# A down projection in which 8 of 22 k-tile pairs are multiplied as 2x2 blocks with seven products

## The chip, the cores and the metric

The kernel runs on one core of a Trainium2 chip. The metric is device time of one execution in microseconds (us), here the median of three runs. Engines are named as in the profile: PE is TensorE, PEld its weight loads, DVE VectorE, ACT ScalarE, POOL GpSimd, and SP the engine that issues most DMAs.

## The reference

A decoder trunk of two layers on 256 tokens with 2048 channels. Each layer has a token mixer and a SwiGLU feed-forward part (D_FF = 5632), each between two norms. What matters here is the feed-forward part, the last step of each layer:

```python
def swiglu(u, w_gu, w_down):
    gu = u @ w_gu
    return (jax.nn.silu(gu[..., :D_FF]) * gu[..., D_FF:]) @ w_down
...
        x = x + rmsnorm(o, g[1])
        x = x + rmsnorm(swiglu(rmsnorm(x, g[2]), ffn_w_gu[l], ffn_w_down[l]), g[3])
```

With h = silu(..) * (..) of shape 256 x 5632, the down projection is h @ w_down, 256 x 5632 times 5632 x 2048, once per layer.

## The kernel before

**Precision.** Every large product is taken in three matmuls. A float32 number is split into hi, its rounding to the type float32r, and lo, the rest, and a product is hi*hi + lo*hi + hi*lo. ACT writes hi (line 193), DVE subtracts to get lo (line 194). For the activations this is done when they are produced (class `XT`, which holds one page for each pair of k-tiles, with hi and lo of both); for the weights it is done as they stream through.

**Weight units.** All weights are cut in units of 128 x 1024 float32 (512 KB), listed in the order of use by `_unit_list`. `take` hands out the next unit as a pair of pages (hi, lo). Before that it issues, in the program's order, what lies ahead: `dma_one` loads a unit on SP's queue into a "raw" page, `split_one` turns a raw page into hi and lo and frees it. `take` starts a load while fewer than three (at its end four) raws are unsplit and `room(1)` holds, and up to two splits while at most `look` units are ahead (4 in layer 0's feed-forward part, 8 in layer 1's) and `room(2)` holds. `room(n)` asks for `st["res"] + n` free pages; `res` is 2 in the gate/up part and 0 in the down projection. Where nothing was split ahead, `take` splits the unit at that moment, behind everything already queued on ACT and DVE.

**Pages and banks.** There are 44 pages of 4 KB per partition. The free list is first in, first out, so a new tile takes the page that has been free for longest, and its first writer waits on the chip for that page's last reader. PSUM has eight banks, kept in the same way.

**Side work.** Matmul loops call `tick` twice after each three matmuls of a unit of the feed-forward part (eight ticks per unit). `tick` advances generators that were handed to `spawn`; a `yield n` puts one off by n ticks. All engines execute in the program's order, so what a generator emits between two units stands between them in the queues of ACT, DVE and PE.

**The feed-forward part** is `ffn`. X (tile `xf`, 8 pages) is the normed x. Gate/up: for each of 22 pairs f2 of k-tiles of h, eight units of `x_unit` (2 k-tiles x 2 row blocks x 3 matmuls, 128 x 512 columns each) fill two banks, and `gu_evac` is spawned: Silu on ACT (799), the product on DVE (801), eight ticks later four transposes (808), two ticks later hi and lo of the pair in `hT` (812, 813). The first two pairs share one loop. Then X is freed and the down projection runs over four chunks c of 512 columns. For each it takes 22 units, one for each pair, into two banks (row blocks t = 0, 1). `Tail.chunk` evacuates a chunk: on ACT a Square with its row sum (563), on DVE the product with the gain row into `og` (567). The gain rows `gb` (two pages) come over POOL's queue. In the last chunk pages of hT are dropped one by one, `step(u)` runs layer 0's preparation of the next stage (memory rows loaded on POOL's queue, new tiles for the next X), and the last four units (`HOLD`) are taken together, so that row block 0 is finished ahead of row block 1 (`Tail.last`). `rstd_of` makes the norm's factor (DVE, then POOL), `Tail.residual` adds to x (597), and in layer 1 `store` writes the output.

**x.** The residual stream x is four pages of 128 x 1024 float32. It stays in SBUF all the time. `next_x` adds the residual of row block 1, transposes x into the next X, and squares x for the next norm.

## Time and profile before

| | |
|---|---|
| median of three runs | 2556.76 us (2556.6 to 2558.26) |
| the profiled execution, its own time | 2556.86 us |
| its span | 2555.1 us |
| mean granted clock of TensorE | 0.997 |
| matmuls of the two down projections | 704 in each of lines 330, 331, 332 |

The span goes from the first to the last instruction; the rest of the execution's time lies around it. A row of the profile's groups reads: line, engine, operation, output<-inputs, shapes, count | busy us, mean ns | idle time of the engine just ahead of them, and what ended it. In rows of a timeline the first number is the start in us, the second the length; a bracket gives the idle time ahead and its releaser. In rows of waits the engine and line on the left waited for those on the right: us in total, times, longest us.

### The profile page before, as it was taken

To read this page: it belongs to the slowest core of one execution; us is meant where nothing else is said; L and a number is where in the kernel's file an instruction comes from. 1 tells how busy PE (TensorE), PEld (TensorE's weight loads), DVE (VectorE), ACT (ScalarE), POOL (GpSimd) and SP (SyncE) were. 2 spreads that over 40 slices of the span, in tenths; PEclk is the share of its full clock that TensorE was granted. 3 is DMA by queue.
4 is the path that set the end of the run, shared out by engine and by line. 5 is a ranking of instruction groups with operands and counts; after the bars stand their busy time and mean duration, and the time that the engine had idled before them with its cause. 6 is when DMAs were issued, how large, how long until landed. Compare 5 with 4: busy or idle time off the path is not lost.

```text
span 2555.1 us, 32090 instructions
## 1 busy us (share of the span) xinstructions
PE 2522.1 (99%) x12326; PEld 2137.7 (84%) x12326; DVE 1449.6 (57%) x1926; ACT 1203.3 (47%) x1704; POOL 58.5 (2%) x73
## 2 busy tenths in 40 slices
PE   8999999999999999999999999999899999999998
PEld 6899999988888888888888888888788888888887
DVE  8564655557445554444457866896544444444444
ACT  7444444456434444444445555565444444444442
POOL 5000000000000000000000000000000000000000
PEclk9999999999999999999999999999999999999999
DMA  8455555576555555566676675346455555556664
GB/s 305 148 181 173 166 166 173 172 246 223 177 183 181 185 187 170 173 209 192 194 233 216 220 245 193 116 142 235 158 175 181 181 174 173 181 173 219 193 190 156
DMA packets 136010, 482.84 MB, mean 189 GB/s; under 512 B 15408, under 2 KB 15408, under 8 KB 135856
## 3 DMA queue, kind: packets, MB, share of 16 engines
q1 hardware_dynamic: 131904, 468.67, 56.8%
q0 software_dynamic: 3232, 11.01, 1.3%
q8 instruction: 96, 1.57, 0.3%
q10 hardware_dynamic: 720, 1.11, 0.1%
q14 instruction: 58, 0.48, 0.1%
HBM read 478.63 MB, written 2.10 MB: 188 GB/s over the span
## 4 chain that ended last, share of the span: by engine, by line
PE 93%; DVE 4%; ACT 2%; issue 1%; DMA 0%; POOL 0%; SPq 0%; DVEq 0%; ACTq 0%; POOLq 0%
PE bk L331 23%; PE bk L332 23%; PE bk L330 23%; PE bk L295 12%; PE bk L297 6%; DVE lo L194 2%; ACT hi L193 1%; PE sk L808 1%; PE sk L500 1%; PE bk L939 1%; PE bk L938 1%; PE sk L540 0%; PE bk L294 0%; PE sk L1123 0%; DVE x L597 0%
## 5 line engine op out<-in xcount | busy, mean ns | idle before, releaser
L194 DVE TENSOR_TENSOR lo<-raw,hi 128x1024 fp32r<-128x1024 f32 (+2 forms) x899 | 1061.6, 1205 | 613.0 <-ACT hi L193 575.6
L193 ACT ACTIVATE hi<-raw 128x1024 fp32r<-128x1024 f32 (+2 forms) x899 | 906.9, 1039 | 499.5 <-PE bk L331 239.3
L330 PE MATMUL bk<-hi,xf 128*128 128x512 f32 x1408 | 554.0, 393 | 0.6 <-ACT xf L383 0.6
L332 PE MATMUL bk<-lo,xf 128*128 128x512 f32 x1408 | 549.3, 390 | 0.0
L331 PE MATMUL bk<-hi,xf 128*128 128x512 f32 x1408 | 548.9, 390 | 0.0
L295 PE MATMUL bk<-xT,hi 128*128 128x512 f32 x1104 | 398.7, 404 | 0.0
L332 PEld LDWEIGHTS bk<-lo,xf 128*128 128x128 f32 x1408 | 265.0, 188 | 55.7
L330 PEld LDWEIGHTS bk<-hi,xf 128*128 128x128 f32 x1408 | 265.1, 188 | 54.1 <-ACT xf L383 1.0
L331 PEld LDWEIGHTS bk<-hi,xf 128*128 128x128 f32 x1408 | 265.3, 188 | 53.5 <-DVE xf L384 0.2
L297 PE MATMUL bk<-xT,lo 128*128 128x256 f32 x1035 | 289.6, 280 | 0.0
L330 PE MATMUL bk<-hi,hT 128*128 128x512 f32 x704 | 274.1, 389 | 0.0
L332 PE MATMUL bk<-lo,hT 128*128 128x512 f32 x704 | 273.9, 389 | 0.0
L331 PE MATMUL bk<-hi,hT 128*128 128x512 f32 x704 | 273.9, 389 | 0.0
L295 PEld LDWEIGHTS bk<-xT,hi 128*128 128x128 f32 x1104 | 204.1, 188 | 39.8 <-issue 0.2
L297 PEld LDWEIGHTS bk<-xT,lo 128*128 128x128 f32 x1035 | 195.5, 189 | 3.1
L331 PEld LDWEIGHTS bk<-hi,hT 128*128 128x128 f32 x704 | 132.2, 188 | 27.6
L330 PEld LDWEIGHTS bk<-hi,hT 128*128 128x128 f32 x704 | 132.2, 188 | 27.3
L332 PEld LDWEIGHTS bk<-lo,hT 128*128 128x128 f32 x704 | 132.2, 188 | 27.3
L801 DVE SCALAR_TENSOR_TENSOR ev<-bk,r_f,ev 128x256 f32<-128x256 f32 x88 | 42.2, 483 | 136.7 <-ACT ev L799 127.8
L799 ACT ACTIVATE ev<-bk,r_f 128x256 f32<-128x256 f32 x88 | 41.5, 474 | 164.9 <-PE bk L332 163.8
L322 ACT ACTIVATE ev<-bk 128x256 f32<-128x256 f32 x93 | 35.5, 382 | 129.7 <-PE bk L295 129.6
L295 PE MATMUL bk<-kT,hi 128*128 128x512 f32 x256 | 91.6, 399 | 0.0
(210 smaller groups left out, 2486.6 us busy)
## 6 DMA issues: line engine op xcount, KB each, us to landing
raw<-in_gu SPq DMA_DIRECT2D x352, 512.0 KB, 3.6
raw<-in_dn SPq DMA_DIRECT2D x176, 512.0 KB, 4.3
raw<-in_a_qk SPq DMA_DIRECT2D x96, 512.0 KB, 4.0
raw<-in_a_v SPq DMA_DIRECT2D x64, 384.0 KB, 3.0
raw<-in_cw SPq DMA_DIRECT2D x32, 512.0 KB, 4.6
raw<-in_b_out SPq DMA_DIRECT2D x32, 512.0 KB, 3.7
raw<-in_a_out SPq DMA_DIRECT2D x24, 512.0 KB, 4.4
raw<-in_b_q SPq DMA_DIRECT2D x24, 512.0 KB, 3.7
```

The source lines that it names most:

```text
L193: nc.scalar.activation(hi[1][:, s], r[:, s], AF.Copy)
L194: nc.vector.tensor_tensor(out=lo[1][:, s], in0=r[:, s], in1=hi[1][:, s].bitcast(F32), op=OP.subtract)
L295: mm(pt[:, :], lhsT=hi[:, ks], rhs=X.hl(kt), start=first, stop=last)
L297: mm(pt[:, S:], lhsT=lo[:, ks], rhs=X.part(kt, 0), start=False, stop=False)
L322: nc.scalar.activation(t1, pt[1][:, S:], AF.Copy)
L330: mm(p[:, :w], lhsT=xh, rhs=u[0][1][:, ws], start=f, stop=False)
L331: mm(p[:, :w], lhsT=xl, rhs=u[0][1][:, ws], start=False, stop=False)
L332: mm(p[:, :w], lhsT=xh, rhs=u[1][1][:, ws], start=False, stop=l)
L500: mm(s[:, o:o + n], lhsT=q[1][:, g, t * P:(t + 1) * P], rhs=k[1][:, g, :n], start=True, stop=True)
L799: nc.scalar.activation(g, pts[t][1][:, :S], AF.Silu, scale=r)
L801: nc.vector.scalar_tensor_tensor(h, pts[t][1][:, S:], r, g, op0=OP.mult, op1=OP.mult)
L808: nc.tensor.transpose(p[:, k * S + t * P:k * S + (t + 1) * P], hs[t][:, k * P:(k + 1) * P], ident)
```

## The change

Of the 22 pairs of k-tiles, the last 8 (`DN_S`, pairs 14 to 21) are multiplied differently. For two column chunks at a time (`cp`, a half of the columns) such a pair is a product of 2x2 blocks: two row blocks by two k-tiles, times two k-tiles by two column chunks. It is computed with seven block products P1 to P7 in place of eight (each is still three matmuls), from sums of blocks on both sides.

- On the activations' side `s_parts` makes four sums of 128 x 128 blocks from the transposes' bank at the end of `gu_evac`, splits them, and keeps them in one more page per pair (`Sp`) until the second half is through.
- On the weights' side a pair and half need the units of both chunks (kinds "a" and "b") and two combined units made on DVE ("T13", "T24"). `split_one` makes hi and lo of the unit a, one page with hi and lo of a half of b, and the pages T13 and T24 from differences and sums.
- The seven products are summed over all eight pairs in banks P1 to P7. The 14 other pairs add to P2 and P4 (chunk a) and to P3 and Q (chunk b), so eight banks are in use. After the last block step `sums` combines the banks on DVE into four SBUF tiles (two pages `ut`), and `block` adds P2, P3, P4 or Q to them ahead of the Square and the gain product, which now read SBUF.
- The order of units in a half mixes block steps with plain steps (`_dn_steps`): in the first half a0 to a4, then pair 14, and so on with two or three plain steps between two block steps, and six plain steps behind the last; in the second half a0 to a3 first, mostly two plain steps between two block steps, and ten behind the last, of which the last four are held as before.
- x is written to DRAM in `next_x` ahead of the feed-forward part (four DMAs on SP), its pages are freed, and it is read back at steps 8 to 11 of the second half. `og` and `gb` pages are taken when first needed, `Sp` and hT pages are dropped one by one in the second half. `res` is 3 in the down projection.

The diff, cut to its core:

```diff
+DN_S = tuple(range(14, FT // 2))
...
+    std = [u for u in range(FT // 2) if u not in DN_S]
+    a, b, q = [("a", u) for u in std], [("b", u) for u in std], [("S", u) for u in DN_S]
+    if cp == 0:
+        head, mix, tail = a[:4], [e for p in zip(a[4:], b) for e in p] + b[len(a) - 4:], []
+        tail, mix = mix[-4:], mix[:-4]
+    else:
+        head, mix, tail = a[:3], a[3:] + b[:6], b[6:]
+    return head + _weave(mix, q, 0) + tail
...
     def split_one():
...
+        if kd == "b":
+            ai, ra = kept["T24"]
+            hl = pages.get([P, UNIT], F32R, "hl", True)
+            split_ap(r[:, Bk], hl[1][:, A], hl[1][:, Bk])
+            ti, t = pages.get([P, UNIT], F32, "t13", True)
+            nc.vector.tensor_tensor(out=t[:, A], in0=r[:, A], in1=ra[:, A], op=OP.subtract)
+            nc.vector.tensor_tensor(out=t[:, Bk], in0=r[:, Bk], in1=r[:, A], op=OP.subtract)
...
+        if kd == "T13":
+            ai, ra = kept["T24"]
+            nc.vector.tensor_tensor(out=ra[:, A], in0=r[:, Bk], in1=ra[:, A], op=OP.add)
+            nc.vector.tensor_tensor(out=ra[:, Bk], in0=ra[:, Bk], in1=ra[:, A], op=OP.subtract)
...
         for s in halves(u, w):
-            nc.scalar.activation(hi[1][:, s], r[:, s], AF.Copy)
-            nc.vector.tensor_tensor(out=lo[1][:, s], in0=r[:, s], in1=hi[1][:, s].bitcast(F32), op=OP.subtract)
-        pages.put(ri, True)
+            split_ap(r[:, s], hi[1][:, s], lo[1][:, s])
+        if kd == "a":
+            kept["T24"] = (ri, r)
+        else:
+            pages.put(ri, True)
...
+        if name == "f":
+            for i in range(4):
+                nc.sync.dma_start(out=x_out[i], in_=x[i][1])
+                pages.put(x[i][0])
...
+    def s_parts(A):
+        sv = tmp.tile([P, 4, P], F32, tag="sv", name="sv")
+        sp = pages.get([P, 4, 2, P], F32R, "sp")
+        tt = nc.vector.tensor_tensor
+        s1 = tmp.tile([P, P], F32, tag="s11", name="s11")
+        nc.scalar.activation(s1, A[:, 0, 1], AF.Copy)
+        tt(out=sv[:, 0], in0=A[:, 1, 1], in1=s1, op=OP.add)
+        tt(out=sv[:, 1], in0=sv[:, 0], in1=A[:, 0, 0], op=OP.subtract)
+        tt(out=sv[:, 2], in0=A[:, 0, 0], in1=s1, op=OP.subtract)
+        tt(out=sv[:, 3], in0=A[:, 1, 0], in1=sv[:, 1], op=OP.subtract)
+        yield 1
+        nc.scalar.activation(sp[1][:, :, 0, :], sv, AF.Copy)
+        nc.vector.tensor_tensor(out=sp[1][:, :, 1, :], in0=sv, in1=sp[1][:, :, 0, :].bitcast(F32), op=OP.subtract)
+        return sp
...
+        if f2 in DN_S:
+            Sp[f2] = yield from s_parts(p.rearrange("p (k t q) -> p k t q", k=2, t=2))
         banks.put(b)
...
-        st["res"] = 0
+        st["res"] = 3
...
+            def quad(u):
+                A, Bk = slice(0, 512), slice(512, 1024)
+                sp = [[Sp[u][1][:, j, i, :] for i in range(2)] for j in range(4)]
+                w = take(f"dn{l}")
+                prod("P1", act(2 * u, 0), w[0][1][:, A], w[1][1][:, A])
+                prod("P2", act(2 * u + 1, 0), w[0][1][:, Bk], w[1][1][:, Bk])
+                give(w)
+                w = take(f"dn{l}")
+                prod("P3", sp[3], w[0][1][:, A], w[0][1][:, Bk])
+                give(w)
+                w = take(f"dn{l}")
+                prod("P5", sp[0], w[0][1][:, A], w[1][1][:, A])
+                prod("P7", sp[2], w[0][1][:, Bk], w[1][1][:, Bk])
+                give(w)
+                w = take(f"dn{l}")
+                prod("P6", sp[1], w[0][1][:, A], w[1][1][:, A])
+                prod("P4", act(2 * u + 1, 1), w[0][1][:, Bk], w[1][1][:, Bk])
+                give(w)
...
+            def sums():
+                yield 12
+                tp = [pages.get([P, 2, 512], F32, "ut") for _ in range(2)]
...
+                nc.scalar.activation(s1, bk["P1"][1], AF.Copy)
+                tt(out=u2, in0=bk["P6"][1], in1=s1, op=OP.add)
+                tt(out=u3, in0=bk["P7"][1], in1=u2, op=OP.add)
+                yield 2
+                tt(out=v, in0=bk["P5"][1], in1=u3, op=OP.add)
+                tt(out=u2, in0=bk["P5"][1], in1=u2, op=OP.add)
...
+            def block(key, pre=None):
+                c, t, s_ = T["c"][key]
+                nc.vector.tensor_tensor(out=s_, in0=bk[key][1], in1=s_, op=OP.add)
+                free(key)
+                tail.rows(2 * cp + c, t, s_, pre)
...
+                    if 8 <= steps < 12:
+                        i = steps - 8
+                        x[i] = pages.get([P, 1024], F32, "x")
+                        nc.sync.dma_start(out=x[i][1], in_=x_out[i])
...
+            if cp == 0:
+                tail.gain(1)
+                spawn(blocks_of(("P2", "P3", "P4", "Q")))
+            else:
+                last_units(plan[-HOLD:])
```

`prod` issues the three matmuls of one product and calls `tick` twice. `tail.rows` is the body of the former `Tail.chunk` for one row block: Square on ACT, the norm's factor where asked for, the gain product on DVE. `blocks_of` waits eight ticks and then emits one `block` per tick; in the second half it handles P2 and P4, and `last_units` handles P3 and Q with the held units.

More of the change, by code (lines that the diff above doesn't have):

```diff
@@ L151, in drop, with drop_one @@
         self.gone += 1
+    def drop_one(self, k2):
+        self.pages.put(self.t[k2][0])
+        self.out.add(k2)
     def release(self):
-        while self.gone < len(self.t):
-            self.drop()
+        for k2 in range(self.gone, len(self.t)):
+            if k2 not in self.out:
+                self.pages.put(self.t[k2][0])
+        self.gone = len(self.t)
 @with_exitstack
@@ L175, in halves, with kind @@
         return (slice(0, w // 2), slice(w // 2, w)) if u == 0 else (slice(0, w),)
+    def kind(u):
+        return units[u][2] if len(units[u]) > 2 else ""
     def dma_one():
-        n, i = units[st["dma"]]
+        n, i = units[st["dma"]][:2]
+        if kind(st["dma"])[:1] == "T":
+            st["dma"] += 1
+            return
         w = a[n].shape[2]
@@ L211, in take @@
         for _ in range(0 if st["quiet"] else 2):
-            while st["dma"] < min(st["split"] + NRAW, n) and room(1):
+            while st["dma"] < n and len(raws) < NRAW and room(1):
                 dma_one()
@@ L215, in take @@
                 split_one()
-        while not st["quiet"] and st["dma"] < min(st["split"] + 4, n) and room(1):
+        while not st["quiet"] and st["dma"] < n and len(raws) < 4 and room(1):
             dma_one()
@@ L221, in give @@
     def give(u):
-        pages.put(u[0][0], True)
-        pages.put(u[1][0], True)
+        for e in u:
+            pages.put(e[0], True)
     side = []
@@ L253, in until @@
             n += 1
-            assert n < 1000
+            assert n < 1000, (sorted(banks.live.values()), len(pages.free) + len(pages.own), [e[0].__name__ for e in side], [e[0].gi_frame.f_lineno for e in side])
     def drain():
@@ L599, in release @@
         def release(self):
-            for i, _ in self.og:
+            for i, _ in self.og.values():
                 pages.put(i)
@@ L841, in ffn @@
+        pair(0)
+        pair(1)
+        tail.finish()
         H.release()
```

175 lines of the change are left out of this document (145 added, 30 removed).

## The prediction

> **What bounds the kernel now.** I read the page's head, the chain of waits, then the stages in windows, because the change touches only one kind of stage twice.
>
> ```profile
> span 2555.1 us, 32090 instructions
> PE 2522.1 (99%) x12326; PEld 2137.7 (84%) x12326; DVE 1449.6 (57%) x1926; ACT 1203.3 (47%) x1704; POOL 58.5 (2%) x73
> PE 93%; DVE 4%; ACT 2%; issue 1%; DMA 0%; POOL 0%; SPq 0%; DVEq 0%; ACTq 0%; POOLq 0%
> 1116.90:1356.50 239.60, 239.60 (x1061) 198.48 (x1060) 124.16 (x121) 104.85 (x121) 5.40 (x10) 1.00 0.65 206
> 2308.00:2546.60 238.60, 238.54 (x1055) 197.22 (x1053) 113.75 (x101) 95.11 (x101) 0.56 (x1) 1.00 0.60 189
> ```
>
> TensorE bounds everything. The last two rows are the two down projections (start:end, length, then busy time and count of PE, PEld, DVE, ACT, POOL, granted clock, DMA share, GB/s). PE never idles there, DVE is half used, and some 1056 matmuls take 239 us: one each 0.2267 us, a unit of twelve in 2.72. The rows of one matmul say 389 ns; that is its length in the pipeline, not its price.
>
> Who decides when a weight unit is ready? The splits, and behind them the pages:
>
> ```profile
> ACT hi L193 <- PE bk L331: 239.3, 153, 1.7
> ACT hi L193 <- PE bk L332: 213.3, 146, 1.9
> ACT hi L193 <- DMA raw<-in_dn: 13.8, 15, 2.5
> L330 PE MATMUL bk<-hi,hT x704: 388/389/474, 1117.1 to 2545.7; 128*128 128x512 f32 x176
> ...
> 1098.92 0.60 ACT L812 ACTIVATE hT<-sk 128x512 fp32r<-128x512 f32 x1 [3.37 <-PE sk L808]
> 1099.41 1.05 ACT L193 ACTIVATE hi<-raw 128x1024 fp32r<-128x1024 f32 x1
> 1100.98 1.07 ACT L193 ACTIVATE hi<-raw 128x1024 fp32r<-128x1024 f32 x1 [0.52 <-PE bk L332]
> 1103.70 1.06 ACT L193 ACTIVATE hi<-raw 128x1024 fp32r<-128x1024 f32 x1 [1.65 <-PE bk L332]
> ...
> 1116.62 0.47 ACT L799 ACTIVATE ev<-bk,r_f 128x256 f32<-128x256 f32 x1 [3.70 <-PE bk L332]
> 1117.31 0.47 ACT L799 ACTIVATE ev<-bk,r_f 128x256 f32<-128x256 f32 x1 [0.21 <-PE bk L332]
> 1117.68 2.00 ACT L193 ACTIVATE hi<-raw 128x1024 fp32r<-128x1024 f32 x2
> ```
>
> ScalarE waits for PE to release a page, rarely for a DMA. The first down matmul starts at 1117.1, so the last gate/up group (pair 21, units 0 to 7) starts at 1117.1 - 8 x 2.72 = 1095.3. Counting pages by the rules of the code (44; 8 for xf, 4 for x, 1 for mv, one per pair in hT; a split ahead needs 2 + 2 free; first freed, first reused), unit 5 of this group must get a page that unit 2 leaves, at 1095.3 + 8.2 = 1103.5: the row 1103.70 is that split, 0.2 us later. So the count describes this machine, and I use it for the changed code.
>
> **The change part by part.**
>
> *Matmuls removed.* 8 pairs x 2 column halves x one product of three matmuls = 48 per layer, 96 in all, x 0.2267 = **-21.8 us**. Certain if nothing else is late.
>
> *Pages at the end of gate/up.* The change frees x (4 pages) but adds an Sp page for each pair from 14 on. When pair 21 runs in layer 0, 44 - 8 - 1 - 21 - 7 = 7 are left where 44 - 8 - 4 - 1 - 21 = 10 were; layer 1 has one more in both. With 10, a split is issued one unit ahead (row 1099.41 for unit 3 stands behind the hT copy, while unit 1 runs). With 7 or 8, three raws and the unit in use leave less than 4 free, so nothing is split ahead: the split of unit 2 is issued only when unit 2 is taken, behind the evacuation of pair 20, which now has s_parts at its end. Durations:
>
> ```profile
> L194 DVE TENSOR_TENSOR lo<-raw,hi 128x1024 fp32r<-128x1024 f32 x833 | 1003.4, 1226 | 613.0 <-ACT hi L193 575.6 <-PE bk L331 28.4 <-issue 1.4
> L193 ACT ACTIVATE hi<-raw 128x1024 fp32r<-128x1024 f32 x833 | 857.0, 1055 | 499.5 <-PE bk L331 239.3 <-PE bk L332 213.3 <-DVE lo L194 17.0
> L323 DVE TENSOR_TENSOR ev<-bk,ev 128x256 f32<-128x256 f32 x93 | 39.2, 422 | 91.5 <-ACT ev L322 90.8
> L567 DVE TENSOR_TENSOR og<-bk,gb 128x512 f32<-128x512 f32 x32 | 22.0, 688 | 24.3 <-ACT junk L563 23.8
> L563 ACT ACTIVATE junk<-bk 128x512 bf16<-128x512 f32 x32 | 19.1, 597 | 81.4 <-PE bk L332 80.8
> L597 DVE SCALAR_TENSOR_TENSOR x<-og,r_o,x 128x512 f32<-128x512 f32 x19 | 14.0, 800 | 0.5
> 1099.55 0.69 DVE L813 TENSOR_TENSOR hT<-sk,hT 128x512 fp32r<-128x512 f32 x1 [3.48 <-ACT hT L812]
> 1118.76 2.36 DVE L194 TENSOR_TENSOR lo<-raw,hi 128x1024 fp32r<-128x1024 f32 x2 [0.47 <-ACT hi L193]
> ```
>
> hT is done on DVE at 1100.24. The four adds of 128 columns cost 0.29 each (422 at 256 columns, 688 at 512: 266 per 256): 1101.45. ScalarE's copy of sv (512 columns, 0.60): 1102.1. Then unit 2: hi 1.06, lo 1.23, ready at 1104.4. Its third matmul, the first to read lo, was due at 1095.3 + 5.44 + 0.45 = 1101.2: **3.2 late**. In pair 20 (9 or 10 pages, one unit ahead) the same chain falls on unit 3, due at an equivalent 1103.95: **0.5 late**. Earlier pairs have two units ahead and hide it. Then the first down unit: today its split (seen before 1116.62) stands ahead of the Silu instructions; with none ahead it stands behind them, as the next one does today: hi from 1117.68, lo from 1118.76 in half of 2.36, done at 1119.95, due at 1117.55: **2.4 late**. 6.1 per layer, **+12.2**. The price if the evacuation were issued elsewhere: zero for all three.
>
> *Down projection, inside a column half.* A block step takes 21 x 0.2267 = 4.76 us of PE. On DVE it costs three full lo (1.226) and five ops of 512 columns (half lo, four sums; nearest row 0.688, highest 0.80): 7.1; on ScalarE 3 x 1.055 + 0.60 = 3.8. Between blocks stand two or three plain units. With two: PE 2 x 2.72 + 4.76 = 10.2, DVE 2 x 1.226 + 7.1 = 9.6. It fits, closely. By pages (12 in layer 0, 13 in layer 1, 3 kept back) the split of T13 in layer 0 takes the pages of the unit just before the block: 0.2 + 1.06 + 1.23 = 2.5 us after the block starts, needed at 2.04 + 0.45: 0.07 late, x 8 = **+0.6**. The four sums behind the last block (2.8 us of DVE) run beside six plain units (16.3 us of PE, 7.4 of DVE), before the next half needs their banks: 0. Ends: 0, and with ops of 0.80 and handoffs of 0.05 the group is 10.6 on DVE, 0.4 late in each of 32 blocks: 13. I take the nearest row's.
>
> *Between the column halves.* The banks of the first half are read by four pairs of DVE instructions (add 0.69, multiply 0.68), queued during unit 1 of the second half, while ut, og and a second gb take pages. Layer 0, from the half's start: nothing is split ahead, so unit 2's split queues behind the blocks. lo of unit 1 ends at 1.4, the first og page is the one unit 0 leaves at 2.9, the blocks end at 7.7 with the last Square (0.60), hi of unit 2 at 8.8, lo at 10.0; due at 5.9: 4.1 late. In the first block the differences wait for the page of the unit before it (0.2 after its start), then two of them, two sums and the lo of T13 take 4 x 0.69 + 1.23: 4.2, due at 2.5: 1.7 late; the unit behind splits into pages that T13 leaves: 0.8 late. Layer 1 has one page more: unit 2 is ahead, unit 3 is 1.8 late, T13 1.2. Together **+9.6**. Bounds: 0 (another split slips ahead) to 14 (layer 1 as bad as layer 0).
>
> *Ends.* The last bank now passes an add before its Square:
>
> ```profile
> 2546.64 0.60 ACT L563 ACTIVATE junk<-bk 128x512 bf16<-128x512 f32 x1 [4.81 <-PE bk L332]
> 2547.36 0.21 DVE L358 TENSOR_SCALAR s<-ssq,s 128x1 f32<-128x1 f32 x1 [1.80 <-ACT junk L563]
> PE sk L608 <- DVE x L597: 0.7, 1, 0.7
> ```
>
> Everything behind 2546.64 shifts by 0.69 and a handoff: 0.75. After layer 0 the third row (waits of PE from 1300 to 1420) shows PE already waiting for x, so it pays too: **+1.5**.
>
> *x to memory and back.* Four stores in next_x and four loads at steps 8 to 11 of the second half, on SP, the weights' own queue. Each waits for nothing that is still open (x was written long before), but shifts the weights behind it.
>
> ```profile
> raw<-in_dn SPq DMA_DIRECT2D x176, 512.0 KB, 4.3
> raw<-in_gu SPq DMA_DIRECT2D x352, 512.0 KB, 3.6
> ```
>
> With a DMA share of 0.60 to 0.65 and three raws (8 us) issued ahead, 4 x 512 KB hide: 0. Uncovered, four transfers at half of 3.6 us would be 7 per burst, 28 in all; the row that matters is the 13.8 us above that ScalarE waited for weights without PE waiting once. I take 0. The row loads on POOL's queue are not moved.
>
> *Clock.* Waits this long have a second price:
>
> ```profile
> 1819.50 0.55 PE L608 MATMUL sk<-cst,x 128*128 128x128 f32 x3 [2.15 <-DVE x L597]
> 1821.03 0.63 PE L331 MATMUL bk<-hi,xf 128*128 128x512 f32 x1
> 1823.59 0.57 PE L331 MATMUL bk<-hi,xf 128*128 128x512 f32 x1
> 1816.00:1820.00 4.00, 1.85 (x11) 1.41 (x12) 2.84 (x5) 1.91 (x4) 0.00 (x0) 1.00 0.00 0
> 1820.00:1824.00 4.00, 4.00 (x13) 3.13 (x12) 2.24 (x5) 2.84 (x6) 0.00 (x0) 0.57 0.92 308
> 1391.60 0.32 PE L371 MATMUL sk<-cst,r_x 128*128 128x128 f32 x1 [1.52 <-POOL r_x L359]
> 1391.00:1393.00 2.00, 0.93 (x5) 0.70 (x6) 1.35 (x4) 2.00 (x5) 1.54 (x3) 1.00 0.08 33
> ```
>
> After 4 us in which PE worked 1.85, the granted clock was 0.57: matmuls 0.43 apart for about 3 us, some 1.5 us lost. A wait of 1.52 cost nothing. Five of my stalls (3.2 twice, 2.4 twice, 4.1) lie above that: 0 to 7.5. I take the two of 3.2, **+3.0**, since the 2.4 are broken by matmuls that need only hi and the 4.1 is one case.
>
> The Trainium skill (TensorE: Matmul & The Clock Gate, "Why this matters for your kernels") warns of idle gaps over about 3 us, after which the clock halves; this case's 2.15 us wait after thin work was enough. By that rule the two of 3.2 and the 4.1 would pay, and the sum would be 1.5 us higher.
>
> Sum: -21.8 + 12.2 + 0.6 + 9.6 + 1.5 + 0 + 3.0 = **+5.1**. The profiled execution took 2556.86 us, 0.1 from the median 2556.76, so 2562.0.
>
> **The rivals.**
>
> *A: splitters not late (the other side).* If the sums of s_parts and the blocks finish in PE's shadow, because a split is issued ahead of them at each place after all, only the first down unit's 2.4 x 2 stays: -21.8 + 4.8 + 0.6 + 1.5 = -14.9: 2542. It decides at one more free page at pair 21 and at the halves. For it: DVE is 57% busy. Against: row 1099.41, whose place behind hT is what the count gives.
>
> *B: DVE bounds the block stretches.* 9.6 of 10.2 leaves 6%. If the 512-column ops cost 0.80, 32 blocks add 13 to the forecast: 2574. For it: the L597 row; against: L567 with 0.688 has the new ops' form.
>
> *C: the x traffic shows.* One burst of four at 7 us, uncovered: 2569. For it: one queue; against: PE's waits name no DMA.
>
> **How the numbers follow.** Forecast 0.65, A 0.14, B 0.16, C 0.05. The forecast's own range is 2556 to 2568: the clock term at 0 to 7.5, the halves -3 to +4. A measurement here can tell about 0.2%, 5.1 us, from no change, so the forecast stands on the upper edge of that: of its 0.65 I give 0.33 to slower, 0.31 to the same, 0.01 to faster; A gives 0.11 to faster and 0.03 to the same; B all and C 0.03 to slower. Faster 0.12, same 0.36, slower 0.52. The range 2552 to 2575 leaves out most of A and the top of B.
>
> **What would show it.** PE waiting for ACT hi and DVE lo in pair 21 (unit 2), at the first down unit, and about 6 us into each second half; down stages of some 238 and 233 us in place of 239; each gate/up stage longer by some 4 us; granted clock under 1 behind the longest waits. PE without waits there would be A; waits at each block, with DVE back to back, B; waits on DMA, C. The prediction fails if the down stages keep the full 10.9 us each, or if blocks wait each time.

## The result and the profile after

The changed kernel takes 2571.57 us (median of four runs, 2570.08 to 2573.35); the kernel before took 2556.68 beside it (2555.91 to 2558.26). The ratio is 1.0058, with a 95% interval of 1.004 to 1.0075: slower by 14.9 us, where 5.1 were forecast. The direction held, and so did the range of 2552 to 2575. The forecast's own range, 2556 to 2568, did not: 2571.57 lies 3.6 above it, in the part that stood there for the rivals B and C, which the runs below refuse as the main cause. That the range held is in part luck; the size is almost three times the forecast.

First the head of the page and the two down projections in windows (columns as before: start:end, length, busy time and count of PE, PEld, DVE, ACT, POOL, granted clock, DMA share, GB/s).

```profile
span 2568.3 us, 32470 instructions
PE 2512.2 (98%) x12230; PEld 2121.7 (83%) x12230; DVE 1623.4 (63%) x2230; ACT 1257.5 (49%) x1804; POOL 59.9 (2%) x73
1124.40:1363.90 239.50, 234.21 (x1012) 190.56 (x1012) 199.46 (x235) 126.56 (x154) 5.70 (x10) 0.99 0.64 211
2326.20:2558.40 232.20, 230.24 (x1012) 189.22 (x1012) 192.72 (x219) 122.59 (x138) 1.40 (x2) 1.00 0.62 203
```

96 matmuls fewer (12326 to 12230), and yet the span is 13.2 longer. Layer 0's down projection, where PE never idled, now has 5.3 us without work and a clock of 0.99; layer 1's comes out as forecast. What PE waits for (view of the waits: in total, times, longest):

```profile
PE bk L398 <- ACT hi L231: 10.7, 3, 6.0
PE bk L954 <- ACT hi L231: 6.7, 5, 2.9
PE bk L956 <- DVE lo L232: 3.6, 7, 0.7
PE bk L363 <- ACT hi L231: 2.5, 1, 2.5
```

L398 and L400 are gate/up matmuls, L954 and L956 those of the down projection, L363 those of the stage behind it; L231 and L232 are the splits. Of the first row, 6.0 is a wait at the start of the program that the kernel before had too. Every other wait for a split is new. In the order of time (start, duration, instruction; in brackets the idle time ahead of it and what ended it):

```profile
1104.10 0.50 PE L398 MATMUL bk<-hi,xf 128*128 128x512 f32 x1 [2.37 <-ACT hi L231]
1105.36 0.80 PE L400 MATMUL bk<-lo,xf 128*128 128x512 f32 x1 [0.53 <-DVE lo L232]
1124.39 0.50 PE L954 MATMUL bk<-hi,hT 128*128 128x512 f32 x1 [1.51 <-ACT hi L231]
1125.65 0.79 PE L956 MATMUL bk<-lo,hT 128*128 128x512 f32 x1 [0.53 <-DVE lo L232]
1250.23 0.50 PE L954 MATMUL bk<-hi,hT 128*128 128x512 f32 x1 [2.92 <-ACT hi L231]
1251.49 0.73 PE L956 MATMUL bk<-lo,hT 128*128 128x512 f32 x1 [0.53 <-DVE lo L232]
1262.15 0.50 PE L956 MATMUL bk<-lo,sp 128*128 128x512 f32 x1 [0.68 <-DVE lo L232]
1366.54 0.50 PE L363 MATMUL bk<-mT,hi 128*128 128x512 f32 x1 [2.54 <-ACT hi L231]
1367.80 0.58 PE L365 MATMUL bk<-mT,lo 128*128 128x256 f32 x1 [0.76 <-DVE lo L232]
```

Pair 21's unit 2, the first down unit, the turn of the column halves and its first block, as foretold; and a fifth place that was not, the stage behind layer 0's down projection. Between 1130 and 1250, and from 1266 to 1363, the trace has no wait of PE at all: the block stretches run clean. Behind each long wait stands the clock (windows of six microseconds):

```profile
1104.00:1110.00 6.00, 5.37 (x16) 4.03 (x17) 2.45 (x2) 1.71 (x3) 0.00 (x0) 0.72 0.00 0
1124.00:1130.00 6.00, 5.09 (x17) 3.83 (x18) 4.66 (x4) 3.28 (x4) 0.00 (x0) 0.72 1.01 396
1250.00:1256.00 6.00, 5.24 (x15) 3.84 (x16) 3.50 (x3) 2.40 (x4) 0.00 (x0) 0.72 0.31 91
1366.00:1372.00 6.00, 4.70 (x17) 3.91 (x18) 3.53 (x4) 3.31 (x5) 0.80 (x1) 0.72 0.68 253
2304.00:2310.00 6.00, 3.68 (x9) 2.47 (x10) 3.63 (x6) 2.52 (x3) 0.00 (x0) 0.72 0.28 90
2326.00:2332.00 6.00, 5.27 (x24) 4.08 (x25) 5.82 (x6) 4.54 (x6) 0.00 (x0) 1.00 0.88 325
```

Five times the same 0.72: 6 x 0.28 = 1.7 us of full speed gone in each, 3.4 us at half. The last row is the first down unit of layer 1, with the same waits (1.51 and 0.52) as the second row, and there the clock stays at 1.00.

Windows of six us hide a pattern that the trace has. Up to the last matmul, every stretch of half speed is one or two steps of 3.41 us long, and within one execution all of them lie on one grid of such steps. In the changed kernel they begin at 1104.82, 1125.30, 1251.59, 1367.65, 1818.20 and 2306.31, which are 6, 37, 34, 132 and 143 steps apart; the one at 1818.20 has two steps, the others one. The two first down units differ by the place of their waits in this grid (the step ahead of the half speed in layer 0, and the step that holds the same wait in layer 1):

```profile
1121.89:1125.30 3.41, 1.72 (x7) 0.78 (x5) 1.90 (x3) 2.86 (x5) 0.00 (x0) 1.00 0.95 346
2323.38:2326.79 3.41, 1.90 (x8) 1.05 (x6) 1.57 (x3) 2.53 (x4) 0.00 (x0) 1.00 0.96 333
```

In layer 0 the step holds the first wait and a part of the second, and PE works 1.72 us of it. In layer 1 the second wait falls wholly into the next step, and PE works 1.90. The last section has the count over all runs.

The span by stretches, from the first and last down matmuls (hT) and the last output matmul of the stage between the layers (oT). The forecast's clock term, 3.0, had no place of its own.

| stretch | before | after | difference | forecast |
|---|---|---|---|---|
| start to layer 0's first down matmul | 1117.1 | 1124.4 | +7.3 | +6.1 |
| layer 0's down projection | 239.6 | 239.2 | -0.4 | -3.7 |
| from there to the last oT matmul | 444.2 | 449.8 | +5.6 | +0.75 |
| from there to layer 1's first down matmul | 505.7 | 512.8 | +7.1 | +6.1 |
| layer 1's down projection | 239.6 | 232.0 | -7.6 | -7.9 |
| end | 8.9 | 10.1 | +1.2 | +0.75 |
| clock | | | (in the rows above) | +3.0 |
| sum | 2555.1 | 2568.3 | +13.2 | +5.1 |

### The profile page after: what moved, and what is told of

The parts are those of the page before. It is cut to its first block, busy times and chain, and to the rows that moved or that the text cites. A ratio compares the mean times of both kernels' runs of the same rounds, so it can differ in the third digit from the quotient of the medians.

```text
span 2568.3 us, 32470 instructions
## 1 busy us (share of the span) xinstructions
PE 2512.2 (98%) x12230; PEld 2121.7 (83%) x12230; DVE 1623.4 (63%) x2230; ACT 1257.5 (49%) x1804; POOL 59.9 (2%) x73
## 3 DMA queue, kind: packets, MB, share of 16 engines
HBM read 482.82 MB, written 6.29 MB: 190 GB/s over the span
## 5 line engine op out<-in xcount | busy, mean ns | idle before, releaser
L232 DVE TENSOR_TENSOR lo<-raw,hi 128x1024 fp32r<-128x1024 f32 (+2 forms) x899 | 1048.7, 1205 | 360.7 <-ACT hi L231 327.9
L231 ACT ACTIVATE hi<-raw 128x1024 fp32r<-128x1024 f32 (+2 forms) x899 | 891.7, 1036 | 237.3 <-PE bk L400 131.6
L398 PE MATMUL bk<-hi,xf 128*128 128x512 f32 x1408 | 554.9, 394 | 5.3 <-ACT hi L231 4.7
L400 PE MATMUL bk<-lo,xf 128*128 128x512 f32 x1408 | 550.4, 391 | 1.5 <-DVE lo L232 1.4
L363 PE MATMUL bk<-xT,hi 128*128 128x512 f32 x1104 | 398.7, 404 | 0.0
L398 PEld LDWEIGHTS bk<-hi,xf 128*128 128x128 f32 x1408 | 265.6, 189 | 59.5 <-ACT hi L231 5.6
L400 PEld LDWEIGHTS bk<-lo,xf 128*128 128x128 f32 x1408 | 265.3, 188 | 59.2 <-DVE lo L232 3.5
L363 PEld LDWEIGHTS bk<-xT,hi 128*128 128x128 f32 x1104 | 204.0, 188 | 39.8 <-issue 0.2
L954 PE MATMUL bk<-hi,hT 128*128 128x512 f32 x544 | 213.5, 392 | 6.4 <-ACT hi L231 6.4
L956 PE MATMUL bk<-lo,hT 128*128 128x512 f32 x544 | 213.6, 393 | 2.4 <-DVE lo L232 2.4
L955 PE MATMUL bk<-hi,hT 128*128 128x512 f32 x544 | 212.7, 391 | 0.0
L954 PEld LDWEIGHTS bk<-hi,hT 128*128 128x128 f32 x544 | 103.0, 189 | 29.2 <-ACT hi L231 8.1
L956 PEld LDWEIGHTS bk<-lo,hT 128*128 128x128 f32 x544 | 102.8, 189 | 25.9 <-DVE lo L232 4.6
L955 PEld LDWEIGHTS bk<-hi,hT 128*128 128x128 f32 x544 | 102.8, 189 | 21.3
L391 DVE TENSOR_TENSOR ev<-bk,ev 128x256 f32<-128x256 f32 x93 | 39.3, 423 | 91.5 <-ACT ev L390 90.8
```

Of the source, the lines that this page charges most:

```text
L231: nc.scalar.activation(hi, src, AF.Copy)
L232: nc.vector.tensor_tensor(out=lo, in0=src, in1=hi.bitcast(F32), op=OP.subtract)
L363: mm(pt[:, :], lhsT=hi[:, ks], rhs=X.hl(kt), start=first, stop=last)
L398: mm(p[:, :w], lhsT=xh, rhs=u[0][1][:, ws], start=f, stop=False)
L400: mm(p[:, :w], lhsT=xh, rhs=u[1][1][:, ws], start=False, stop=l)
L954: mm(p, lhsT=xh, rhs=wh, start=f, stop=False)
```

## The experiments

The theory at this point: all waits are splits issued too late, for want of pages, and what the forecast lacks is the stage behind layer 0 and a bigger price of the clock. The rivals were that DVE or the traffic of x sets the pace. Of e1 to e7 and e12 there is one execution each. Runs e1 to e4 were timed beside 2556.77 of the kernel before, e5 to e8 beside 2556.61, e9 to e11 beside 2557.48.

**e1: no reserve of pages ahead of the held units.**

```
             drain()
+            st["res"] = 0
             us = [take(f"dn{l}") for _ in range(HOLD)]
```

> Edit: the reserve of 3 free pages ends ahead of the last four units of each down projection. The changed kernel took 2571.6 us; behind layer 0's down projection PE waits 2.54 + 0.76 us for the first unit of the next stage and its clock drops after it. Theory (no page left above the reserve, so nothing of the next stage is split ahead and the split queues behind the last Square): both waits go, PE waits for x instead as before (0.7 plus up to 0.8 for the new add), the clock stays at 1.00: 3 to 5 us faster, 2567 to 2568.5. Rival (the added add and Square in front of the next stage are the price, whatever is split ahead): the 2.5 us wait stays, 2571 to 2572.

2569.61. The wait that it was to remove is still there and longer, so the reserve is not what holds that split back:

```profile
1122.83 0.50 PE L954 MATMUL bk<-hi,hT 128*128 128x512 f32 x1 [1.51 <-ACT hi L231]
1366.06 0.80 PE L363 MATMUL bk<-mT,hi 128*128 128x512 f32 x1 [3.58 <-ACT hi L231]
```

The first row shows where time was won: the first down unit has the same 1.51, but comes 1.56 earlier, since the identical wait in pair 21 was followed by no half speed this time. The price of one and the same wait is not fixed: here the grid cuts the 2.37 in two, and e12 returns to this. The two profiled executions differ by only 0.5 in the span (2568.3 and 2567.8), so most of the 1.56 is lost again further on.

**e2: the extra chains of pairs 19 to 21 held back until the gate/up part is over.**

```
         if f2 in DN_S:
+            while f2 >= 19 and not rf.get("late"):
+                yield 0
             Sp[f2] = yield from s_parts(p.rearrange("p (k t q) -> p k t q", k=2, t=2))
...
         X.release()
+        rf["late"] = True
```

> Edit: s_parts of pairs 19, 20 and 21 wait until xf is released. Theory (pages: with 9 or 10 free in pair 21 a unit is split ahead again): the waits of pair 20 (0.44), of unit 2 of pair 21 (2.37 + 0.53) and of the first down unit (1.51 + 0.53) go in both layers, with them three or four clock drops of about 1.7 us: 14 to 18 us faster, 2553 to 2558. Rival (the length of the s_parts chain on ACT and DVE is the cost, wherever it stands): the three chains now stand together at the start of the down projection and PE waits there instead, 5 us or more of the 12; 2565 to 2572.

2563.07, between the two. The gate/up part is back at 505.4 in layer 1 (before: 505.7), so the chains with their pages do make the late splits there. But they now stand together at the start of the down projection, which grows to 242.7 and 235.4 (after: 239.2 and 232.0), 3.4 a layer:

```profile
1127.14 0.50 PE L957 MATMUL bk<-hi,hT 128*128 128x512 f32 x1 [0.33 <-ACT hi L231]
1131.97 0.50 PE L957 MATMUL bk<-hi,hT 128*128 128x512 f32 x1 [0.99 <-ACT hi L231]
```

**e3: rival B, one difference of every block computed twice on DVE** (32 more instructions of 512 columns).

```
             nc.vector.tensor_tensor(out=t[:, Bk], in0=r[:, Bk], in1=r[:, A], op=OP.subtract)
+            nc.vector.tensor_tensor(out=t[:, Bk], in0=r[:, Bk], in1=r[:, A], op=OP.subtract)
```

> Edit: one of the two differences made for T13 is computed twice (32 more DVE instructions of 512 columns, 0.69 us each). Theory (DVE has slack inside the block stretches, the loss is at the five places): 0 to 4 us slower, where the extra op delays T13 in the blocks that wait already. Rival B of the prediction (DVE bounds the block stretches): each extra op shows in full, 32 x 0.69 = 22 us slower, 2590 or more; half of that would still speak for it.

2577.21, 5.6 above the changed kernel: more than the 0 to 4 expected, but far from 32 x 0.69 = 22 if DVE set the pace. The steady blocks take the extra work without a wait, but for two of 0.19 and 0.44 late in layer 0; otherwise only the first blocks behind the turn of the halves pay, in layer 0 this one (0.29 in the changed kernel):

```profile
1262.56 0.50 PE L955 MATMUL bk<-hi,sp 128*128 128x512 f32 x1 [1.01 <-ACT hi L231]
```

All new waits together come to 1.8 us. Most of the rest is clock: ten steps of half speed ahead of the last matmul, where the changed kernel has seven.

**e4: rival C, x stored twice and read twice** (a second DRAM buffer, four more stores and four more loads a layer).

```
                 nc.sync.dma_start(out=x_out[i], in_=x[i][1])
+                nc.sync.dma_start(out=x_out2[i], in_=x[i][1])
...
+                        nc.sync.dma_start(out=x[i][1], in_=x_out2[i])
                         nc.sync.dma_start(out=x[i][1], in_=x_out[i])
```

> Edit: x is stored to a second place in DRAM too, and read from there first and then from the first: 16 more transfers of 512 KB. Theory (the x traffic is hidden behind raws loaded ahead): within 2 us of 2571.6. Rival C of the prediction (the x traffic delays the weights on their own queue): about as much again as it costs now, 7 us per burst, 2578 to 2599.

2579.92, 8.3 more: past the 2 us expected, and inside rival C's range. The doubled stores make no wait of PE; the doubled reload in layer 0 makes the held units late:

```profile
1354.17 0.79 PE L956 MATMUL bk<-hi,hT 128*128 128x512 f32 x1 [5.36 <-ACT hi L231]
```

PE has no wait at that place in the changed kernel, so its own traffic is hidden from PE; the cover is just not twice as large. In all ScalarE waits 26.2 us for the down projections' weights here, against 6.3 in the changed kernel. In layer 1 PE meets no new wait, but the tail is 13.5 (after: 10.1): three splits near the end wait 4.77, 5.58 and 4.93 for their weights, and VectorE's sums stand behind them in its queue and begin at 2557.13 in place of 2539.42.

**e5: one page more at the handover** (the two partial sums still needed in the second half share one page, so that the other comes free, and the reserve of e1).

```
-                s1, u2, u3, v = (tp[j // 2][1][:, j % 2, :] for j in range(4))
+                s1, u2, u3, v = (tp[j % 2][1][:, j // 2, :] for j in range(4))
...
-                if not T["left"]:
-                    for e in T["pages"]:
+                if cp == 1 and T["left"] in (0, 2) or not T["left"]:
+                    for e in T["pages"][:1 + (cp == 0)]:
                         pages.put(e[0])
+                    del T["pages"][:1]
...
+                st["res"] = 0
                 us = [take(f"dn{l}") for _ in range(HOLD)]
```

> Edit on the changed kernel: in the second half one of the two ut pages is freed behind P2 and P4 and the reserve ends ahead of the last four units, so 5 pages are free there in layer 0 as in the kernel before (4 in the changed kernel, and 4 without the reserve alone). Theory (a split of the next stage needs pages; without them it queues behind the last Square): the waits of 2.54 + 0.76 us behind layer 0's down projection go, 2 to 5.5 us faster by the clock's part, and the first matmul of the next stage follows the last of the down projection within 0.3 us. Rival (the wait belongs to the added add, or to the transfer of the unit): a wait of over 2 us stays there.

2573.01, and the wait stands: 3.58 again. One page does not do it; whether more would, e10 asks.

**e6: as e2, with pair 20's chain put off by 24 more steps of the side work.**

```
+            if f2 == 20:
+                yield 24
             Sp[f2] = yield from s_parts(p.rearrange("p (k t q) -> p k t q", k=2, t=2))
```

> Edit on the changed kernel: s_parts of pairs 19, 20 and 21 wait until xf is released as in the run with late parts, but the three chains stand some one and a half units apart. Theory (pages at the end of gate/up, and the chains hurt only where they stand together ahead of the next split): gate/up of layer 1 stays at 505 us, the two down stages fall from 242.7 and 235.4 us to about 239 and 232, in all 2555 to 2560. Rival (three chains cost PE their length wherever they stand in the down projection): the down stages stay near 242 and 235, 2562 to 2564.

2565.33, a miss. The wait only moves on, into the first block:

```profile
1136.63 0.80 PE L959 MATMUL bk<-hi,sp 128*128 128x512 f32 x1 [1.85 <-ACT hi L231]
```

**e7: the bank sums P2 and P4 already in the first half, beside its last plain units,** with e5's page and no reserve from there to the second half's first block.

```
-                if "a" not in left and "S" not in left and (kd == "a" or kd == "S") and cp == 1:
+                if "a" not in left and "S" not in left and (kd == "a" or kd == "S"):
                     spawn(blocks_of(("P2", "P4")))
             if cp == 0:
-                spawn(blocks_of(("P2", "P3", "P4", "Q")))
+                spawn(blocks_of(("P3", "Q")))
...
                 for key in keys:
                     block(key)
                     yield 1
+                if cp == 0 and "P2" in keys:
+                    tail.gain(1)
+                    st["res"] = 0
...
                     if cp == 1:
                         H.drop_one(u)
+                        st["res"] = 3
```

> Edit on the changed kernel: in the first column half too, P2 and P4 are combined and evacuated beside its last plain units, one ut page is freed behind them, and the reserve is lifted until the first block of the second half is through. Theory (the queue of four blocks and the missing pages make the waits after the change of halves): in layer 0 the waits of 2.92 + 0.53, 0.29 + 0.68 and 0.34 us, in layer 1 those of 0.43 + 0.53 and 0.48 go or shrink to a fifth: 6 to 9 us faster, 2562 to 2566. Rival (the banks and their evacuation bound the change of halves): waits of some 3 us in layer 0 stay, or move into the tail of the first half.

2565.03: 6.5 less. In layer 0 the wait at the turn falls from 2.92 to 0.49, and its down projection from 239.2 to 234.9. Another 2.4 come from behind layer 0, where the wait of 2.54 is still there but costs no half speed this time; that is mostly the grid's doing and not the edit's. The turn:

```profile
1250.70 0.50 PE L954 MATMUL bk<-hi,hT 128*128 128x512 f32 x1 [0.49 <-ACT hi L231]
1251.96 0.50 PE L956 MATMUL bk<-lo,hT 128*128 128x512 f32 x1 [0.53 <-DVE lo L232]
```

**e8: e5, e6 and e7 together.**

> The three edits together (ut page and reserve at the end, late and spread parts, halves). Theory (all that the change lost, but for the add at the ends and some 1.5 us in the layer between, is in these places and the clock behind them): 2556.8 - 21.8 + 1.5 + 1.5 + 1 to 4 = 2539 to 2543, faster than before by 0.5 to 0.7%. If DVE or the x traffic held the rest: over 2548.

2559.73 (2559.15 to 2561.36), ratio 1.0012 with an interval of 1.0003 to 1.0021: not the 2539 to 2543 expected. e6's wait in the first block (1.86) and the one behind layer 0 (3.58) were still there. Moving chains about does not remove their pages; the next three runs leave every chain where it is and free pages.

**e9: the pages of x's k-tiles given back one by one during pair 21,** and not eight at once behind it.

```
-  x_unit(p, f"gu{l}", X, 2 * u, 512, u == 0, u == KT // 2 - 1)
+  x_unit(p, f"gu{l}", X, 2 * u, 512, u == 0, u == KT // 2 - 1, fs[0] == FT // 2 - 1)
```

> Edit: while the last gate/up pair (21) runs, each of its eight units gives back the page of x k-tiles that it has read last, instead of all eight pages after the pair; nothing is moved in order, no chain waits. Theory (the three late splits at the end of gate/up come from a shortage of pages alone, eight of which the x k-tiles hold until the last matmul): the waits of TensorE at pair 21 unit 2 (2.37 + 0.53), at pair 20 (0.44) and at the first down unit (1.51 + 0.53) go, with the half-speed windows behind them; the first down matmul at about 1117.3 instead of 1124.4, gate/up of layer 1 some 505.5 long instead of 512.8, the down stages unchanged at 239.2 and 232.0: 2571.6 - 14.4 = about 2557, between 2555 and 2559. Rival (the chains of pairs 19 to 21 are the cause, and they have to stand somewhere): the wait moves into the first units of the down projection as it did when the chains were held back, +3 a layer: 2562 to 2564.

2555.89 (2554.22 to 2557.30), 15.7 below the changed kernel. The first down matmul comes at 1118.0 and layer 1's gate/up is 507.2 long. From pair 20 to the turn of the halves layer 0 has left of its waits only

```profile
1081.80 0.50 PE L400 MATMUL bk<-lo,xf 128*128 128x512 f32 x1 [0.44 <-DVE lo L232]
1104.73 0.50 PE L400 MATMUL bk<-lo,xf 128*128 128x512 f32 x1 [0.41 <-DVE lo L232]
```

The chains did not wander into the down projection (236.9 and 231.1). So the shortage of pages, and not the chains, was the cause there. What layer 1's gate/up keeps, 1.5 above the kernel before, is mostly the same two short waits.

**e10: the eight pages for the next stage's activations taken after layer 0's feed-forward part,** not from step 10 of its second half on.

```
-        if u >= 10:
-            Xk.grow()
...
+    while len(Xk.t) < KT // 2:
+        Xk.grow()
     spawn(next_x(tail, x, Xk, 6, rb, "x"))
```

> Edit: the eight pages for the next stage's activations (kT1) are taken after layer 0's feed-forward part and not from step 10 of its second column half on; nothing else. Theory (the wait of TensorE at the handover to the next stage's projection, 2.54 + 0.76, is a late split for want of pages: kT1's eight and x's four stand beside the held units' eight): the wait goes, layer 0's held units and the first projection run on without one: 2571.6 - 3.6 = about 2568, 2566 to 2569.5. Rival (the split stands behind the last Square on ScalarE for its order of issue, and pages have no part in it): the same wait, 2570 to 2573.

2565.60 (2564.27 to 2566.75), 6.0 less where 3.6 were expected. ScalarE near the handover, first in the changed kernel, then in e10:

```profile
1364.82 0.63 ACT L633 ACTIVATE junk<-ut 128x512 bf16<-128x512 f32 x1 [4.78 <-DVE ut L1007]
1365.45 1.99 ACT L231 ACTIVATE hi<-raw 128x1024 fp32r<-128x1024 f32 x2
```

```profile
1352.15 1.99 ACT L231 ACTIVATE hi<-raw 128x1024 fp32r<-128x1024 f32 x2
1357.52 0.63 ACT L633 ACTIVATE junk<-ut 128x512 bf16<-128x512 f32 x1 [3.38 <-DVE ut L1007]
1363.03 0.63 ACT L633 ACTIVATE junk<-ut 128x512 bf16<-128x512 f32 x1 [4.78 <-DVE ut L1007]
1363.65 1.99 ACT L231 ACTIVATE hi<-raw 128x1024 fp32r<-128x1024 f32 x2
```

In the changed kernel the next stage's first split stands behind the last Square, which waits for the last bank (1364.82 to 1366.54, PE idle 2.54). With eight pages more a split of the next stage is done in front of both Squares; PE goes through, and waits only later, 1.50 for x. The clock stays at 1.00 where it was 0.72, and the stretch up to the last oT matmul falls from 449.8 to 445.1.

**e11: e7, e9 and e10 together, the reserve back from the second half's second block on.**

> Edit: the two edits above, and that of the run with P2 and P4 also in the first column half, with the reserve of pages back only after the second block of the second half. Theory (every loss but the clock's is a late split for want of pages): no wait of TensorE over 0.6 between pair 19 and the next stage, gate/up 505.5, down stages 231 to 234 in both layers: 2565.0 (that run) - 14.4 - 3.6 = 2547, 2543 to 2551, faster than the kernel before (2556.7) by 0.2 to 0.5%. Rival (the down projection's own blocks need the slack, and a gain in one place comes back in the next, as in the run with all the earlier edits at once): 2555 to 2562.

2546.20 (2545.84 to 2547.23); the ratio to the kernel before is 0.9956, interval 0.9942 to 0.9969: faster than both. The head and the down projections:

```profile
span 2545.4 us, 32463 instructions
1118.60:1352.00 233.40, 230.87 (x1012) 188.11 (x1011) 199.62 (x237) 127.05 (x156) 6.29 (x11) 1.00 0.67 224
2303.90:2535.30 231.40, 230.17 (x1012) 188.91 (x1012) 189.33 (x217) 119.66 (x137) 1.89 (x3) 1.00 0.60 199
```

Behind the program's start its waits for splits are all under 0.75, and the clock is 1.00 in both down stages. Of the 21.8 us of saved matmuls it keeps 2555.1 - 2545.4 = 9.7 in the span. Of the rest some 7 stay in the two down projections, 3 in the stretches that end in them, and 2 behind them.

**e12: the clock's price by itself, in the kernel before.**

```
+    late = {}
+    for q in range(2):
+        g0 = units.index((f"gu{q}", 0))
+        late.update({g0 + 8 * (4 + 2 * k) + 4: 4 + k for k in range(8)})
...
             nc.scalar.activation(hi[1][:, s], r[:, s], AF.Copy)
+            for _ in range(late.get(u, 0)):
+                nc.vector.tensor_tensor(out=lo[1][:, :512], in0=r[:, :512], in1=r[:, :512], op=OP.subtract)
```

> Edit: the kernel before, not the changed one; in each layer's gate/up, at unit 4 of the pairs 4, 6, ... 18, VectorE does 4, 5, ... 11 subtractions of 512 columns that nobody uses (some 0.7 each) ahead of the unit's lo part, so that TensorE meets eight waits a layer of rising length, some 15 apart or more, in a stretch that has none otherwise; the result is unchanged. It measures the term of the clock by itself. Theory from the traces so far (the changed kernel and its variants: 2.37 + 0.53 idle cost from nothing to 2.8 more at half speed behind it, 1.51 + 0.53 from nothing to 1.9, waits up to 1.2 nothing): waits up to 1.2 are followed by no half speed, those of 1.5 to 3.5 by it in more than half of the cases, and the loss is between 0 and 3 for one and the same length, so that the moment decides and not the length alone. Rival (the prediction's term: only waits near 3 and above, and then 1.5 each): no half speed behind waits under 2.5, and nearly the same loss, about 1.5, behind each that is longer. Total: 2556.7 + the waits (from none to about 5 each, some 30 to 45 in all) + the clock's 8 to 15: 2590 to 2615.

2575.67 beside 2558.16, below the 2590 to 2615 expected. Fewer waits arose than planned, because the shorter delays were hidden; five lone ones of 1.21 to 3.34 are left, and each is followed by a steady run of matmuls. Rows of PE, then the steps of this run's grid around the first three:

```profile
944.64 1.29 PE L815 MATMUL sk<-cst,ev 128*128 128x128 f32 x4 [1.98 <-DVE ev L808]
993.68 0.94 PE L815 MATMUL sk<-cst,ev 128*128 128x128 f32 x4 [2.62 <-DVE ev L808]
1049.68 0.50 PE L339 MATMUL bk<-lo,xf 128*128 128x512 f32 x1 [2.65 <-DVE lo L201]
2189.54 0.94 PE L815 MATMUL sk<-cst,ev 128*128 128x128 f32 x4 [1.21 <-DVE ev L808]
2237.85 1.22 PE L815 MATMUL sk<-cst,ev 128*128 128x128 f32 x4 [3.34 <-DVE ev L808]
```

```profile
941.30:944.72 3.42, 1.44 (x8) 0.86 (x6) 3.25 (x6) 0.00 (x0) 0.00 (x0) 1.00 0.00 0
944.72:948.13 3.41, 3.41 (x10) 2.69 (x11) 2.67 (x4) 1.54 (x2) 0.00 (x0) 0.50 0.70 222
989.09:992.50 3.41, 1.97 (x9) 1.31 (x7) 3.20 (x5) 0.00 (x0) 0.00 (x0) 1.00 0.35 127
992.50:995.92 3.42, 2.18 (x11) 1.74 (x12) 2.15 (x4) 1.26 (x2) 0.00 (x0) 1.00 0.00 0
995.92:999.33 3.41, 3.41 (x17) 2.82 (x16) 3.06 (x4) 2.29 (x3) 0.00 (x0) 1.00 0.47 129
1047.12:1050.53 3.41, 0.85 (x4) 0.72 (x5) 3.27 (x4) 0.87 (x1) 0.00 (x0) 1.00 0.46 154
1050.53:1053.94 3.41, 3.41 (x10) 2.64 (x9) 3.14 (x4) 2.37 (x4) 0.00 (x0) 0.50 0.00 0
```

1.98 us of idle time cost the clock, 2.62 did not, 2.65 did. So the length alone does not decide, and the limit near 3 that the forecast used is not there. The steps show what does. The 1.98 lies in one step, of which PE works 1.44, and so does nearly all of the 2.65, with 0.85; the next step runs at half speed. The 2.62 is cut by the grid, PE works 1.97 and 2.18 of the two steps, and the clock stays. The 3.34 leaves PE 0.45 of its step and costs a step at half speed; the 1.21 leaves 2.13 and costs none.

## Why the prediction was right and wrong

**Right: the pages, and where they bite.** By the trace the waits, with the restart of PE, are 3.2 at pair 21, 2.4 at the first down unit and 0.6 at pair 20; the forecast had 3.2, 2.4 and 0.5. At layer 0's turn of the halves it had 4.1, 1.7 and 0.8 against 3.8, 1.3 and 0.5 measured, in layer 1 1.8 and 1.2 against 1.3 and 0.6: 7.5 in all for a term of 9.6, so that the term of the halves was 2.1 too large and hides as much of the miss. e9 shows the cause by undoing it alone; e7 takes most of layer 0's waits at the halves away (4.8 us of them to 2.0; layer 1's stay, 1.4 to 1.2), but with three edits at once (blocks earlier, a page, the reserve), whose shares stay open. T13's 0.07 in each steady block does not show. (The sum's own terms give 235.9 and 231.7 for the two down projections without the clock, and not the 238 and 233 that the prediction's list of signs names; 239.2 and 232.0 were measured.)

**Right: the rivals refused.** B falls by the wait-free block stretches and by e3, though the first blocks do have little room. C falls because no wait of PE is found at the traffic; e4 shows how near its bound is, in layer 0 by PE's wait and in layer 1 by the late sums. A's point of decision was named as one more free page; with the pages of e7, e9 and e10 the kernel is at 2546, where A had 2542.

**Wrong: the clock term.** The step "I take the two of 3.2, +3.0, since the 2.4 are broken by matmuls that need only hi and the 4.1 is one case" is mis-sized. Five places lost clock: pair 21 in both layers, the first down unit and the turn of the halves in layer 0, which were among its five stalls, and the place behind layer 0, which was not. PE worked 2.88, 3.06, 3.42, 3.26 and 3.31 us in the five steps of half speed, and half of that, 8.0, was lost: 5 us more than the term. (Behind the stage between the layers both kernels lose 3 to 4 us more, so that is not new.) The error was to look for a length that decides, and to count one wait for a long one and two short ones for none: 1.51 + 0.53 at the first down unit cost a step at half speed in layer 0 and nothing in layer 1. Its bound (7.5) was about right; the value should have been taken from the middle of the bounds or above. The Trainium skill's rule (TensorE: Matmul & The Clock Gate, "Why this matters for your kernels", gaps over about 3 us) fits e12's 3.34 and the turn of the halves in layer 0 (2.92, then 0.53); it does not cover 1.51 + 0.53 at the first down unit nor e12's 1.98 and 2.65, which lost clock too. Here the measurement decides.

**Wrong: the ends.** "Everything behind 2546.64 shifts by 0.69 and a handoff: 0.75", and the same after layer 0. At the end 1.2 were measured. After layer 0 the step looked at the row where PE waits for x, and not at the page count there, although it had counted pages at every other place: kT1's eight and x's four pages stand beside the eight parts of the held units, so the next stage's first split slides behind the last Square. It cost 2.54 + 0.76 of idle time and half-speed matmuls, and with them gone that stretch is 4.7 shorter (e10).

These terms do not close the account of the 8.1 us between +5.1 and the +13.2 of the spans; three to four are left. A part is that PE runs empty and starts again: behind a wait at full speed the first two matmuls start 0.335 us apart in place of 0.2267, a tenth for each of nearly twenty waits. The rest, most of it behind layer 0, was not followed up. The median lies 1.5 above the profiled execution (2570.08), which was the fastest of four; the four ran at a mean clock of 0.994, 0.994, 0.993 and 0.992 in the order of their times, so at least part of that, too, goes with the clock.

## What to carry to other kernels

Where work is cut from the bounding engine, and the cut needs buffers, count the free buffers at every seam that the change touches, the one behind it included: here most of the microseconds lost stood where a split had no page to go to, and giving pages back a few microseconds earlier was worth 15.7 us without moving one instruction of the chain. Give a freed buffer to the lookahead before you reorder anything; reordering the chains (e2) won 8.5 us and carried the other part of the waits to the next seam. And price a wait of TensorE by its length and by the grid of 3.41 us: in these traces idle time under 1.5 us in a step cost its length alone, and over 1.9 us in one step cost a step at half speed too, 1.7 us with PE busy. As the grid lies elsewhere in every execution, a lone wait between 1.5 and 3.7 us (twice 1.87) pays with a chance only, and short waits that stand close together add up.

## What was not expected of the hardware

After a wait of TensorE the granted clock mostly did one of two things: nothing, or half speed for one step of 3.41 us (behind five places of the changed kernel and three of the five waits of e12). In e4 there was also a longer drop, of two steps, behind the same 2.37 + 0.53 at layer 1's pair 21:

```profile
2311.49:2314.90 3.41, 2.88 (x8) 2.20 (x8) 1.83 (x2) 0.29 (x1) 0.00 (x0) 0.50 0.03 5
2314.90:2318.31 3.41, 3.41 (x10) 2.67 (x9) 0.41 (x1) 1.06 (x1) 0.00 (x0) 0.50 0.22 50
```

Half of PE's 6.29 busy us there, 3.1, was lost. Whether a drop came did not follow from the length of the wait: 1.51 + 0.53 us of idle time at the first down unit left the clock at 1.00 in e4's layer 0 and halved it in the changed kernel's; 2.62 and 2.65 in e12 went opposite ways. It did follow from the idle time within the steps of the grid. In the 14 traces (before, after, e1 to e12), from 12 us on and up to the last matmul, 70 steps at full speed were followed by half speed, and each of them left PE without a matmul for at least 1.52 us. Another 10252 were followed by full speed, and none of them left PE idle for more than 1.87. In between both occur, so the limit, near half of a step, is not sharp in what the traces count as idle. The grid lies differently against the program in each of the 14 executions, which is why one and the same wait has several prices, and fits that runs of one kernel differ by some us. What sets the grid, and what decides on a second step at half speed, stays open.
